# A hybrid encoder layer on one core: attention's steps spread wider, linear attention's set closer, and rests issued a step behind

## The chip, the core and the metric

The kernel runs on one core of a Trainium2 chip. The core has five engines that run side by side, each through its own queue in order: TensorE (PE in the profile, with its weight loads as PEld), VectorE (DVE), ScalarE (ACT), GpSimd (POOL) and SyncE (SP). The last two issue DMA transfers here; POOL also fills a few tiles. Engines wait for each other through semaphores. The metric is device time in microseconds from start to end of one execution; before the change it is 2229.53 us, the median of 3 runs (2229.45 to 2230.32).

## What is computed

One layer over 512 tokens with 2048 features, all in 32-bit floats. Half of the mixing width is attention with three (window, dilation) patterns merged by their softmax denominators (16 heads of 64), the other half gated linear attention in both directions (4 heads, keys of 128, values of 256). Then an output projection, a SwiGLU block and norms.

```python
h = rmsnorm(x, attn_norm_w[l])
proj = h @ w_in[l]
aq, ak, av, gq, gk, gv, gr, glr = jnp.split(proj, split_idx, axis=-1)
attn = mixture_of_dilations(_heads(aq, 16), _heads(ak, 16), _heads(av, 16), rel_bias_table)
log_a_f = jax.nn.log_sigmoid(lr_f @ gla_gate_w_fwd[l] + gla_gate_b_fwd[l]) / 16.0
...
o = gla_causal(qh, kh, vh, log_a_f) + flip(gla_causal(flip(qh), ..., flip(log_a_b)))
o = o * lax.rsqrt(jnp.mean(o * o, axis=-1, keepdims=True) + 1e-6)
gla_out = (_merge_heads(o) * gla_norm_w[l]) * jax.nn.silu(gr)
x = x + jnp.concatenate([attn_out, gla_out], axis=-1) @ w_out[l]
h = rmsnorm(x, ffn_norm_w[l])
x = x + (jax.nn.silu(h @ w_gate[l]) * (h @ w_up[l])) @ w_down[l]
```

## The kernel before

Every large product is made in a rounded 32-bit format in three passes. An operand is split into a rounded part (a cast, on ScalarE) and a rest (operand minus rounded part, on VectorE), and TensorE multiplies rounded by rounded, rounded by rest and rest by rounded (L321 to L323, or L330 to L332).

**Weights** come through the `Stream`. SP loads pieces of 128 x 1024 from `in_w_in` and other weights (L207); a piece is two halves of 512 columns. `split` makes the rounded part (L222) and the rest (L223) of each half ahead of its use, gives the raw piece back after its second half, and loads the next. At most three raw pieces are held.

**Jobs.** A job is one projection of 512 columns: 16 halves, and for each half 12 matmuls of 512 columns into four PSUM banks (four banks, three passes). At the start of half i, `run_job` splits up to half i + 2, so rounded part and rest of a half are issued two halves ahead. At a job's end `evac` empties the four banks: `evac_gqk` (L787, L790, on VectorE), `evac_gv` (L816, on ScalarE), `evac_gr` (L830 on VectorE, L835 on ScalarE, then `gla_out`, L844, on VectorE).

**Six jobs in the middle** make the linear attention's q and k (pair 0), v (pair 0), q and k (pair 1), v (pair 1) and two gates. While they run, smaller work is woven in as generators that yield after every step. `side` holds them in a queue: the low-rank gate product, then attention, then the linear attention of heads 0 and 1 (`two` lets the two alternate), then of heads 2 and 3. A later one begins when the one ahead of it is done. A job's `rate` says how many side steps go with each half; with `fine` set they are spread over the half's four groups of three matmuls. Before every side step one step of `urgent` runs. The rate is 2.9 in all six jobs. `slow` adds an empty step after each step of the low-rank product and of linear attention.

**Attention** goes in 64 units (16 heads, four blocks of 128 queries), two steps a unit, with the stages of five units overlapped. For unit u: scores (TensorE, L593 and L594), add bias and take the extreme (`att_max`, VectorE, L603), exponential with its sum (`att_exp`, ScalarE, L611), reciprocal and scaling (`att_norm`, VectorE, L615 and L616), transposes into PSUM (TensorE, L621), rounding (`att_round`, ScalarE, L629), rest (`att_rest`, VectorE, L635), product with the values (TensorE, L645 and L646, every second unit), a lift and an add (`att_lift`, ScalarE, L655, and `att_mix`, VectorE, L664). When a pair of heads is done, `split_of` splits the result (L387, L388). The 8 PSUM banks are shared: four belong to the job, the rest serve scores, transposes and products in turn.

`read_qk(pr)` has POOL read q and k of a pair of heads back from device memory (`qkd`, L535, eight transfers); `load_qk(pr)` scales and splits them: a ScalarE activation (L547, L552) and a VectorE rest (L548, L553) for each of four tiles, rest right behind its activation.

**Linear attention** of one head has 14 steps: gates (TensorE, L866), for each direction a log-sigmoid (ScalarE L876 to L878, VectorE L879, L880), for each direction a scan and its exponents (VectorE L888 to L903, ScalarE L901) and then scaled q and k (ScalarE L907, L908; VectorE L910, L911), products and transposes of them (TensorE L929, L935; VectorE L940, ScalarE L945, VectorE L949), states (TensorE L963, ScalarE L975, VectorE L977), an empty step, outputs (TensorE L999, ScalarE L1002), normalisation (L358 to L364, L1012 on ScalarE), transposes (TensorE L1018, VectorE L1021).

**Just before the six jobs** the attention's own q and k projections run in another form (`Front`, seven products of half size, L1392 and L1406, with casts L1310 and rests L1315). Its last unit is emptied by `evac7` (nine ScalarE copies, L1432 to L1440, and VectorE adds, L1426 and L1427). At the second of its last four pieces `read_qk(0)` is issued, at the third `load_qk(0)` goes to the head of `urgent`, and a step of `urgent` runs after each piece.

Of the kernel before, what the change touches and what calls it, by code (L numbers as in the profile page):

```python
# [16 lines left out]
F32R = mybir.dt.float32r  # L17
U32 = mybir.dt.uint32
AF = mybir.ActivationFunctionType
OP = mybir.AluOpType  # L20
# [98 lines left out]
def layer(nc, tc, x, attn_norm_w, w_in, rel_table, gw_f, gb_f, gw_b, gb_b, gla_norm_w, w_out,  # L119
# [7 lines left out]
    with tc.manual_schedule(), \  # L127
# [52 lines left out]
        class Stream:  # L180


            def __init__(self):
                self.pieces = []
                self.halves = []
                self.n_dma = self.n_conv = 0
                self.limit = 3
                self.held = 0
                self.until = None
                self.big = None  # L190
                self.keep = 0

            def add(self, pieces):
# [6 lines left out]
            def load(self):  # L200
                last = len(self.pieces) if self.until is None else self.until
                while self.n_dma < last and self.held < self.limit and s4.free:
# [5 lines left out]
                    self.n_dma += 1  # L208

            def split(self, upto):  # L210
                end = len(self.halves) if self.until is None else 2 * self.until
                while self.n_conv < min(upto, end):
                    h = self.halves[self.n_conv]
                    if self.n_dma <= h[0]:
                        self.load()
                    raw = self.pieces[h[0]][1]
                    r = raw.t[:, h[1] * 512:(h[1] + 1) * 512]
                    if self.big is not None and self.n_conv >= self.big and len(s4.free) > 3:
                        h[2], h[3] = s4.pair()
                    else:  # L220
                        h[2], h[3] = hilo(self.keep)
                    act.copy(h[2].t, r)  # L222
                    dve.tensor_tensor(h[3].t, r, h[2].f, op=OP.subtract)  # L223
                    self.n_conv += 1
                    if h[1] == 1:
                        put(raw)
                        self.held -= 1
                        self.load()

# [64 lines left out]
        def run_job(j):  # L294
# [6 lines left out]
            for i in range(j.n):  # L301
# [5 lines left out]
                if j.tail is not None:  # L307
                    j.before(i)
                _, _, wh, wl = st.halves[j.first + i]
                ks = j.kts[i * per:(i + 1) * per]  # L310
# [226 lines left out]
        def load_qk(pr):  # L537


            qs, ks = qkr.pop(pr)  # L540
            sign = (-1.0, 1.0)[pr % 2]
            QK[pr] = []
            for n in range(2):
                v = lambda x_: x_.rearrange("p (b c) -> p b c", c=P)
                e, low = s2.get(F32R), slice(64, 128)
                src, scale = v(qs[n].f)[:, :, ::-1], -sign * DH ** -0.5
                act.activation(v(e.t), src, AF.Copy, scale=scale)  # L547
                dve.scalar_tensor_tensor(v(e.t)[low], src[low], scale, v(e.f)[low], op0=OP.mult, op1=OP.subtract)  # L548
                put(qs[n])
                yield  # L550
                k = s2.get(F32R)
                act.activation(k.t, ks[n].f, AF.Copy, scale=sign)  # L552
                dve.scalar_tensor_tensor(ks[n].t, ks[n].f, sign, k.f, op0=OP.mult, op1=OP.subtract)  # L553
                QK[pr].append((e, k, ks[n]))
                yield
            ready.add(pr)
# [56 lines left out]
        def att_norm(u):  # L613
            L = AT[u]
            dve.reciprocal(ar[u % 4], asum[u % 4])  # L615
            dve.tensor_scalar(L.t, L.t, ar[u % 4], None, op0=OP.mult)  # L616

# [39 lines left out]
        def att_mix(v):  # L657
# [10 lines left out]
            if v % 4 == 3:  # L668
                mixh[pr] = split_of(mixf.pop(pr))

        def attention():
# [5 lines left out]

            for u in range(UNITS + 5):
                h = u // 4
                if u < UNITS:  # L680
# [4 lines left out]
                    while h // 2 not in ready:  # L685
                        run_urgent()
                run(att_scores, u)
                run(att_exp, u - 1)
                run(att_round, u - 3)
# [121 lines left out]
        def evac_gv(pr):  # L811
            def f(banks):
# [305 lines left out]

        def before_first(i):
            if i == 2:  # L1120
                load_v(0)

        n_front = len(jobs)
        RATE = 2.9
        for pr in range(2):
            seg = [(w_in, C_GQ + pr * 256), (w_in, C_GK + pr * 256)]
            job("A", [piece512(seg, None, k) for k in range(0, KT, 2)], list(range(KT)), acts_h,
                evac_gqk(pr), rate=RATE, start=gstart if pr == 0 else None,
                before=None if pr else before_first, limit=3)
            job("B", [piece512(w_in, C_GV + pr * 512, k) for k in range(0, KT, 2)], list(range(KT)), acts_h,  # L1130
                evac_gv(pr), rate=RATE)

        for pr in range(2):
            job("A", [piece512(w_in, C_GR + pr * 512, k) for k in range(0, KT, 2)], list(range(KT)), acts_h,
                evac_gr(pr), rate=RATE)
        n_in = len(jobs)
# [397 lines left out]
        class Front(Feed):  # L1534
# [18 lines left out]
            def run(self):  # L1553
                banks = {}
                for i, (u, q) in enumerate(self.seq):
# [12 lines left out]
                    if u == len(self.units) - 1:  # L1568
# [485 lines left out]
```

## Time and profile before

| | |
|---|---|
| median of 3 runs | 2229.53 us (2229.45 to 2230.32) |
| the profiled execution | 2232.89 us, of which the span of the trace is 2231.1 |
| TensorE busy | 2180.0 us (98%) |
| VectorE busy | 1786.4 us (80%) |
| ScalarE busy | 1180.2 us (53%) |
| GpSimd busy | 332.1 us (15%) |
| mean granted clock of TensorE | 0.993 |

A row of the timeline gives the start in us from the span's start, how long it took, engine, line, operation, what it writes and reads, and how many were merged; in brackets, how long the engine had been idle before and what ended that. A row of the waits gives who waited for whom: us in total, how often, the longest. A row of a stretch gives its length and for each engine the busy time and the number of instructions, then the granted clock of TensorE, the DMA engines' busy share and GB/s. A row of a group gives busy us and the mean ns of one, then idle us of the engine before it and what ended that. Lines such as L593 are those of the kernel before. Matmuls are pipelined, so the busy time of TensorE isn't its peak.

### The profile page before, as it was taken

The numbers are of one execution on the slowest core, as the hardware profiler recorded it, in microseconds if no ns is written. First come the engines' busy times: TensorE is split into PE (matmuls) and PEld (weight loads), VectorE is DVE, ScalarE is ACT, GpSimd is POOL, SyncE is SP. The second block draws the span as 40 slices with busy tenths as digits, with TensorE's granted clock in tenths as the row PEclk, the third lists the DMA queues.
The fourth block names the chain that finished last, engine by engine and source line by source line (L and its number), as shares of the span: only waits on it lengthen the run. The fifth ranks groups of instructions, "written<-read, shape, count | busy, mean of one in ns | idle before, by whom it ended". The sixth has DMA issues, their size and how long they took to land.

```text
span 2231.1 us, 34599 instructions
## 1 busy us (share of the span) xinstructions
PE 2180.0 (98%) x12618; PEld 1907.8 (86%) x12618; DVE 1786.4 (80%) x3104; ACT 1180.2 (53%) x2165; POOL 332.1 (15%) x462
## 2 busy tenths in 40 slices
PE   9999898998999999999999999999999999999998
PEld 7888777777878888988888888888888899999987
DVE  5699668777664676799898999999898888988885
ACT  7454345565554444455555555555555655555562
POOL 0011221110000110012121211212121120011300
PEclk9999999999999999999999999999999999999999
DMA  5367763443323885257767776766777886566982
GB/s 187 123 188 176 188 204 115 143 138 120 124 85 108 306 292 190 86 153 188 179 184 182 174 199 170 190 179 182 182 177 196 242 194 199 184 181 154 276 315 76
DMA packets 257368, 397.81 MB, mean 178 GB/s; under 512 B 18925, under 2 KB 154269, under 8 KB 257198
## 3 DMA queue, kind: packets, MB, share of 16 engines
q1 hardware_dynamic: 203134, 276.69, 38.7%
q0 software_dynamic: 53744, 118.39, 23.8%
q8 instruction: 99, 1.62, 0.3%
q14 instruction: 71, 0.58, 0.1%
q10 hardware_dynamic: 320, 0.53, 0.1%
HBM read 285.37 MB, written 64.29 MB: 157 GB/s over the span
## 4 chain that ended last, share of the span: by engine, by line
PE 54%; DMA 1%; DVE 1%; issue 1%; ACT 0%; POOL 0%; DVEq 0%; POOLq 0%; ACTq 0%
PE ps L1406 24%; PE ps L1392 12%; PE ps L1755 5%; PE ps L1756 5%; PE ps L1754 5%; PE ps L330 1%; PE ps L331 1%; PE ps L332 1%; DMA gd<-b 1%; DMA b<-a 1%; PE ps L1949 0%; PE ps L1948 0%; PE ps L1950 0%; DVE b L1315 0%; DVE a L1625 0%
## 5 line engine op out<-in xcount | busy, mean ns | idle before, releaser
L1310 ACT CAST b<-b 128x768 fp32r<-128x768 f32 (+1 forms) x537 | 489.0, 945 | 335.0 <-DVE b L1315 142.0
L1315 DVE TENSOR_TENSOR b<-b,b 128x768 fp32r<-128x768 f32 (+1 forms) x537 | 563.8, 1084 | 32.4 <-ACT b L1310 20.3
L1406 PE MATMUL ps<-b,b 128*128 128x512 f32 x1552 | 451.0, 393 | 0.4 <-ACT b L1310 0.2
L1406 PE MATMUL ps<-a,b 128*128 128x512 f32 x1248 | 365.6, 394 | 3.3 <-DVE b L1426 3.3
L1406 PEld LDWEIGHTS ps<-b,b 128*128 128x128 f32 x1552 | 263.5, 188 | 30.7 <-ACT b L1310 0.7
L1392 PEld LDWEIGHTS ps<-b,b 128*128 128x128 f32 x1552 | 252.8, 190 | 36.1
L1392 PE MATMUL ps<-b,b 128*128 128x256 f32 x1552 | 275.5, 280 | 0.0
L1392 PEld LDWEIGHTS ps<-a,b 128*128 128x128 f32 x1248 | 208.0, 189 | 34.2 <-DVE b L1315 0.5
L1406 PEld LDWEIGHTS ps<-a,b 128*128 128x128 f32 x1248 | 207.3, 189 | 23.2 <-ACT a L1438 3.8
L1392 PE MATMUL ps<-a,b 128*128 128x256 f32 x1248 | 223.7, 280 | 0.0
L1297 DVE TENSOR_TENSOR b<-b 128x512 f32<-128x512 f32 x244 | 167.4, 686 | 19.0 <-DMA b<-in_w_down_dram 7.1
L1754 PE MATMUL ps<-b,b 128*128 128x256 f32 x624 | 176.6, 283 | 0.0
L1756 PE MATMUL ps<-b,b 128*128 128x256 f32 x624 | 176.6, 283 | 0.0
L1755 PE MATMUL ps<-b,b 128*128 128x256 f32 x624 | 176.6, 283 | 0.0
L223 DVE TENSOR_TENSOR b<-b,b 128x512 fp32r<-128x512 f32 x171 | 114.9, 686 | 69.8 <-ACT b L222 69.8
L330 PE MATMUL ps<-b,b 128*128 128x512 f32 x392 | 156.4, 399 | 2.2 <-ACT b L222 2.2
L331 PE MATMUL ps<-b,b 128*128 128x512 f32 x392 | 154.1, 393 | 0.9 <-DVE b L223 0.9
L332 PE MATMUL ps<-b,b 128*128 128x512 f32 x392 | 154.0, 393 | 0.0
L222 ACT CAST b<-b 128x512 fp32r<-128x512 f32 x171 | 100.8, 618 | 41.8 <-PE ps L332 27.7
L1755 PEld LDWEIGHTS ps<-b,b 128*128 128x128 f32 x624 | 119.8, 192 | 0.0
L1756 PEld LDWEIGHTS ps<-b,b 128*128 128x128 f32 x624 | 119.8, 192 | 0.0
L1754 PEld LDWEIGHTS ps<-b,b 128*128 128x128 f32 x624 | 119.8, 192 | 0.0
(295 smaller groups left out, 4289.8 us busy)
## 6 DMA issues: line engine op xcount, KB each, us to landing
b<-in_w_gate_dram SPq DMA_DIRECT2D x109, 512.0 KB, 4.2
b<-in_w_up_dram SPq DMA_DIRECT2D x88, 512.0 KB, 4.3
b<-in_w_down_dram SPq DMA_DIRECT2D x88, 512.0 KB, 8.0
b<-in_w_in_dram SPq DMA_DIRECT2D x78, 512.0 KB, 3.8
b<-a POOLq DMA_DIRECT2D x150, 256.0 KB, 4.5
b<-in_w_out_dram SPq DMA_DIRECT2D x32, 512.0 KB, 5.7
gd<-b POOLq DMA_DIRECT2D x22, 512.0 KB, 3.9
b<-gd SPq DMA_DIRECT2D x22, 512.0 KB, 8.1
```

Source lines behind the costliest of these rows:

```text
L223: dve.tensor_tensor(h[3].t, r, h[2].f, op=OP.subtract)
L330: mm(o, xh.t[:, c], wh.t[:, w], start=first and not on, stop=False, skip_group_check=on)
L331: mm(o, xh.t[:, c], wl.t[:, w], start=False, stop=False, skip_group_check=on)
L332: mm(o, xl.t[:, c], wh.t[:, w], start=False, stop=last, skip_group_check=on)
L1297: dve.tensor_tensor(s_[:, :, 0:2], r[:, :, 1:3], r[:, :, 0:1].to_broadcast(shape), op=OP.add)
L1310: act.copy(o, src)
L1315: dve.tensor_tensor(o, src, h, op=OP.subtract)
L1392: mm(o, wl, xh, start=False, stop=end, skip_group_check=True)
L1406: mm(o.rearrange("p (s t) -> p s t", s=2), wh, x_, start=first and p == 0, stop=False, skip_group_check=True)
L1754: mm(o, xh[:, t], wh, start=first and h == 0, stop=False, skip_group_check=True)
L1755: mm(o, xh[:, t], wl, start=False, stop=False, skip_group_check=True)
L1756: mm(o, xl[:, t], wh, start=False, stop=last, skip_group_check=True)
```

## The change

1. The six jobs' rate of 2.9 becomes 2.5 for the first four (`RATES[0]`) and 2.0 for the two gate jobs. Linear attention loses the empty steps that `slow` put in; the low-rank product keeps them.
2. `load_qk(0)` goes to the head of `urgent` at the second half of the first job instead of the third of the last four front pieces.
3. In the six jobs (`st.lag = j.fine`) the rest of a weight half is issued by the next step's `split`, ahead of that step's cast, instead of right behind its own cast; the raw piece goes back, and its successor is loaded, a step later.
4. `load_qk` issues each rest a step behind its activation: one activation a step, four steps, the last rest behind the fourth.
5. Odd units' scaling leaves `att_norm` for a new `att_scale` on ScalarE, ahead of the next exponential, in the step before their transposes. Even units' scaling and all reciprocals stay on VectorE.
6. The split of a finished pair of heads moves from `att_mix` to the start of the next unit.

```diff
@@ Stream
+            def rests(self, upto):
+                while self.open and self.open[0] < upto:
+                    n = self.open.popleft()
+                    h = self.halves[n]
+                    raw = self.pieces[h[0]][1]
+                    dve.tensor_tensor(h[3].t, raw.t[:, h[1] * 512:(h[1] + 1) * 512], h[2].f, op=OP.subtract)
+                    if h[1] == 1:
+                        put(raw)
+                        self.held -= 1
+                        self.load()
+
             def split(self, upto):
+                self.rests(len(self.halves))
...
                     act.copy(h[2].t, r)
-                    dve.tensor_tensor(h[3].t, r, h[2].f, op=OP.subtract)
+                    self.open.append(self.n_conv)
                     self.n_conv += 1
-                    if h[1] == 1:
-                        put(raw)
-                        self.held -= 1
-                        self.load()
+                    if not self.lag:
+                        self.rests(self.n_conv)
@@ run_job
+                st.lag = j.fine
+                st.rests(j.first + i + 1)
@@ load_qk
+            for m in range(5):
+                if m:
+                    _, hf, src, lo, scale, r, done = todo[m - 1]
+                    dve.scalar_tensor_tensor(lo, src[r], scale, hf[r], op0=OP.mult, op1=OP.subtract)
+                    if done:
+                        put(done)
+                if m < 4:
+                    act.activation(todo[m][0], todo[m][2], AF.Copy, scale=todo[m][4])
+                    yield
@@ attention
         def att_norm(u):
-            L = AT[u]
             dve.reciprocal(ar[u % 4], asum[u % 4])
-            dve.tensor_scalar(L.t, L.t, ar[u % 4], None, op0=OP.mult)
+            if u % 2 == 0:
+                dve.tensor_scalar(AT[u].t, AT[u].t, ar[u % 4], None, op0=OP.mult)
+
+        def att_scale(u):
+            if u % 2:
+                act.activation(AT[u].t, AT[u].t, AF.Copy, scale=ar[u % 4])
...
-                mixh[pr] = split_of(mixf.pop(pr))
+                at["mix"] = pr
...
+                if "mix" in at:
+                    pr = at.pop("mix")
+                    mixh[pr] = split_of(mixf.pop(pr))
                 run(att_scores, u)
+                run(att_scale, u - 2)
                 run(att_exp, u - 1)
                 run(att_round, u - 3)
@@ evac_gv
-                side.append(slow(two(gla(2 * pr), gla(2 * pr + 1))))
+                side.append(two(gla(2 * pr), gla(2 * pr + 1)))
@@ before_first, jobs
+            if i == 1:
+                urgent.appendleft(load_qk(0))
...
-        RATE = 2.9
+        RATES = (2.5, 2.0)
@@ Front.run
-                            urgent.appendleft(load_qk(0))
```

More of the change, by code (lines that the diff above doesn't have):

```diff
@@ L191, in __init__ @@
                 self.keep = 0
+                self.lag = False
+                self.open = deque()
             def add(self, pieces):
@@ L542, in load_qk @@
             QK[pr] = []
+            v = lambda x_: x_.rearrange("p (b c) -> p b c", c=P)
+            low = slice(64, 128)
+            todo = []
             for n in range(2):
[L544 to L553, printed above, removed]
-                QK[pr].append((e, k, ks[n]))
-                yield
+                e, k = s2.get(F32R), s2.get(F32R)
+                todo += [(v(e.t), v(e.f), v(qs[n].f)[:, :, ::-1], v(e.t)[low], -sign * DH ** -0.5, low, qs[n]),
+                         (k.t, k.f, ks[n].f, ks[n].t, sign, slice(0, 128), None)]
+                QK[pr].append((e, k, ks[n]))
+            for m in range(5):
[7 more added lines that the diff above has]
+                    yield
             ready.add(pr)
@@ L676, in run @@
                     f(u)
-            for u in range(UNITS + 5):
+            for u in range(UNITS + 6):
                 h = u // 4
@@ L1127, in layer @@
             job("A", [piece512(seg, None, k) for k in range(0, KT, 2)], list(range(KT)), acts_h,
-                evac_gqk(pr), rate=RATE, start=gstart if pr == 0 else None,
+                evac_gqk(pr), rate=RATES[0], start=gstart if pr == 0 else None,
                 before=None if pr else before_first, limit=3)
             job("B", [piece512(w_in, C_GV + pr * 512, k) for k in range(0, KT, 2)], list(range(KT)), acts_h,
-                evac_gv(pr), rate=RATE)
+                evac_gv(pr), rate=RATES[0])
         for pr in range(2):
             job("A", [piece512(w_in, C_GR + pr * 512, k) for k in range(0, KT, 2)], list(range(KT)), acts_h,
-                evac_gr(pr), rate=RATE)
+                evac_gr(pr), rate=RATES[1])
         n_in = len(jobs)
```

## The prediction

> **What bounds the kernel now.** I read the page first: its head and engine rows.
>
> ```profile
> span 2231.1 us, 34599 instructions
> PE 2180.0 (98%) x12618; PEld 1907.8 (86%) x12618; DVE 1786.4 (80%) x3104; ACT 1180.2 (53%) x2165; POOL 332.1 (15%) x462
> ```
>
> TensorE (PE) is idle for 51 us of the span, so a change that only reorders work can win that and the time at a lowered clock, no more. Next, the busy time by stretches, cut where the diff acts: the end of the front products, the stage with attention, the one with linear attention alone.
>
> ```profile
> core 0: us, PE busy (x) PEld busy (x) DVE busy (x) ACT busy (x) POOL busy (x), PEclk, DMA share, GB/s
> ...
> 272.00:282.00 10.00, 0.60 (x2) 0.50 (x2) 4.00 (x10) 4.85 (x14) 4.24 (x8) 0.72 1.07 287
> 282.00:288.00 6.00, 5.94 (x17) 4.10 (x16) 5.94 (x11) 3.64 (x8) 0.00 (x0) 0.62 1.04 357
> ...
> 449.00:457.00 8.00, 7.40 (x33) 5.98 (x34) 6.62 (x16) 5.28 (x12) 2.97 (x7) 0.79 0.82 268
> ...
> 540.00:548.00 8.00, 5.00 (x19) 4.12 (x18) 5.25 (x13) 4.09 (x9) 0.00 (x0) 0.66 0.46 182
> ...
> 556.00:724.00 168.00, 165.23 (x797) 138.84 (x796) 94.92 (x174) 87.51 (x193) 7.36 (x14) 1.00 0.34 106
> ```
>
> Then who made TensorE wait, in 306 to 556 us (attention) and in 556 to 724 us (linear attention alone):
>
> ```profile
> PE ps L593 <- DVE b L635: 12.6, 12, 3.0
> PE ps L621 <- DVE a L616: 2.9, 5, 1.0
> PE ps L621 <- ACT b L816: 2.7, 1, 2.7
> PE ps L621 <- DVE a L790: 2.6, 2, 1.8
> ```
>
> ```profile
> PE ps L929 <- DVE a L911: 2.0, 1, 2.0
> PE ps L1018 <- ACT b L1012: 0.7, 2, 0.4
> ```
>
> Three places, then: a hole of over 9 us at 272; 20.8 us of waits in attention, plus clock losses of 0.21 x 8 + 0.34 x 8 = 4.4 us; 2.7 us in linear attention. The rest of the span has little to give.
>
> **Part 1: load_qk(0) goes from the last front products to the second step of the first projection job.** The timeline of ScalarE, and TensorE's row after the hole:
>
> ```profile
> 276.93 0.63 ACT L547 ACTIVATE a<-a 128x512 fp32r<-128x512 f32 x1 [13.60 <-DMA a<-qkd]
> 277.47 0.35 ACT L1432 COPY a<-ps 128x256 f32<-128x256 f32 x1
> ...
> 279.56 0.46 ACT L1440 COPY a<-ps 128x256 f32<-128x256 f32 x1
> 280.25 0.63 ACT L552 ACTIVATE a<-a 128x512 fp32r<-128x512 f32 x1 [0.22 <-DMA a<-qkd]
> 280.78 1.12 ACT L222 CAST b<-b 128x512 fp32r<-128x512 f32 x2
> ```
>
> ```profile
> 271.65 0.39 PE L1392 MATMUL ps<-b,b 128*128 128x256 f32 x2
> 281.44 0.79 PE L321 MATMUL ps<-b,b 128*128 128x512 f32 x1 [9.39 <-ACT b L222]
> ```
>
> ScalarE sits 13.6 us on a DMA that only attention needs; queued behind it are the nine evacuation copies and the first weight cast, for which TensorE waits. In the changed order the copies follow the products bank by bank. The last two still come after 272.05 (0.26 us apart), then the cast (0.62): TensorE resumes near 273.5, idle 1.5 us instead of 9.4: 7.9 saved. Over 282 to 288 it ran 17 matmuls; at full clock, with weight matmuls alone, the view by stretches has
>
> ```profile
> 573.00:589.00 16.00, 16.00 (x72) 13.23 (x72) 15.00 (x28) 7.09 (x17) 1.07 (x2) 1.00 0.33 96
> ```
>
> 72 in 16 us, 0.22 each, 2.7 us for the twelve of a half. The loss of 6 - 17 x 0.22 = 2.2 us goes with the hole. Sum **-10 us**. What is late next: load_qk(0)'s four activations now stand in front of the cast for the fifth half. That cast is needed only after four halves of 2.7 us plus the low-rank matmuls, after 284; the first k read had landed at 280.25. The eight POOL reads are not moved. Bounds: 0 (the reads slip by 6 us) to -11.
>
> **Part 2: attention at 2.5 steps a half, odd scalings on ScalarE, rests a step behind.** What the rate is worth depends on what sets the pace. Three units as the timeline has them (L603 max, L611 exponential, L629 rounding, L635 rest, L222/L223 weight cast and rest):
>
> ```profile
> 403.29 0.68 DVE L603 CUSTOM_DVE_ANT_0 a<-ps,b 128x512 f32<-128x512 f32 x1
> ...
> 404.07 0.72 ACT L611 ACTIVATE a<-a,small 128x512 f32<-128x512 f32 x1 [0.39 <-DVE small L603]
> 404.45 0.16 DVE L615 RECIPROCAL small<-small 128x1 f32<-128x1 f32 x1
> ...
> 404.79 0.57 ACT L629 CAST b<-ps 128x512 fp32r<-128x512 f32 x1
> ...
> 406.38 0.68 DVE L603 CUSTOM_DVE_ANT_0 a<-ps,b 128x512 f32<-128x512 f32 x1
> ...
> 409.51 0.69 DVE L223 TENSOR_TENSOR a<-b,a 128x512 fp32r<-128x512 f32 x1 [1.85 <-ACT a L222]
> ...
> 410.72 0.68 DVE L603 CUSTOM_DVE_ANT_0 a<-ps,b 128x512 f32<-128x512 f32 x1
> ```
>
> This is a ring between two engines: max, exponential (0.78 later), rounding (0.72), rest and next max (0.60 each, the pace of the two instructions from 409.51 to 410.72), 2.7 us with nothing in the way. A weight rest ahead of L635 makes it 3.09 (403.29 to 406.38); one that waits for its cast, queued behind rounding, 4.34 (406.38 to 410.72). The lag takes away these waits, 35 us (20.6 + 14.3), and the scaling leaves VectorE for every second unit:
>
> ```profile
> L616 DVE TENSOR_SCALAR a<-a,small 128x512 f32<-128x512 f32 x64 | 31.2, 487 | 2.3
> L223 DVE TENSOR_TENSOR a<-b,a 128x512 fp32r<-128x512 f32 x33 | 22.7, 689 | 20.6 <-ACT a L222 20.6
> L223 DVE TENSOR_TENSOR b<-b,b 128x512 fp32r<-128x512 f32 x16 | 11.0, 689 | 14.3 <-ACT b L222 14.3
> ...
> L816 ACT ACTIVATE b<-ps,small 128x512 f32<-128x512 f32 x8 | 4.9, 698 | 0.0
> ```
>
> VectorE loses 32 x 0.487 = 15.6 us; ScalarE gains 32 x 0.698 = 22.3 (no activation from SBUF with a column as scale is in the trace; L816, from PSUM, is the nearest). The new activation stands ahead of the next exponential, and for that unit it needs max, mix and reciprocal first: 404.61 instead of 404.07, then 0.62, so that ring takes 2.7 + 1.2 = 3.9. The mean of 2.7 and 3.9 is 3.3, with load_qk and the mix splits some 3.5. TensorE's own unit is 3.4 us of work now (306 to 556 less 25.2, over 64 units and about two of start and end); 2/2.5 - 2/2.9 = 0.11 more halves of 2.7 us in it make 3.7. So TensorE sets the pace, narrowly. The lost time of 20.8 + 4.4 = 25 us should fall to what the job ends cause (L816 and L790: 5.3, part of L593's, some clock): **-18 us**. Bounds: 0 if the ring stays slower than TensorE, -25 if all goes. Releasing raw weights a step later delays SP's next load by one half; three pieces of two halves are held, so I take nothing: two pieces still held, some 11 us of work, hide it (without that cover a cast could come one half, 2.7 us, late).
>
> The Trainium skill's page "ScalarE: Activation LUTs", section "Rules for kernel authors", says to do plain multiplies on VectorE, not ScalarE. The rows agree on price, 487 against 698 ns; by the rule alone the move loses 6.7 us.
>
> **Part 3: linear attention without its empty steps, 2 steps a half.** Here the cover disappears. Its first half, gate to L929, is a chain through ScalarE and VectorE that ends just as TensorE wants it:
>
> ```profile
> 562.97 0.69 ACT L876 ACTIVATE a<-ps,wcol 128x512 f32<-128x512 f32 x1 [0.29 <-PE ps L866]
> ```
>
> ```profile
> 588.03 0.68 DVE L911 TENSOR_TENSOR a<-a,a 128x512 f32<-128x512 f32 x1
> ```
>
> ```profile
> 589.37 1.95 PE L929 MATMUL ps<-a,a 128*128 128x128 f32 x16
> ```
>
> ```profile
> 639.10 0.69 ACT L876 ACTIVATE a<-ps,wcol 128x512 f32<-128x512 f32 x1 [1.60 <-PE ps L866]
> ```
>
> For the first pair of heads (rows at 562, 588 and 589) the chain takes 25.7 us (562.97 to 588.71) and TensorE came to L929 0.66 us after its end. In the changed record seven halves lie between, not nearly ten: 7 x 2.7 + 0.5 = 19.4 us. The chain loses two weight rests (1.2) and a few waits (0.5), but four L816 evacuations of the fourth job, which wait for that job's last matmul, now fall into its ScalarE part: +3.9. So 28 against 19.4: **+8.5 us** of stall. TensorE meets part of it early, since weight rests issued a step later leave one half of slack, not two. The second pair went from 639.10 to the L911 that ends TensorE's wait, around the evacuation of the fifth job:
>
> ```profile
> 669.26 1.16 PE L929 MATMUL ps<-a,a 128*128 128x128 f32 x8 [2.00 <-DVE a L911]
> ```
>
> Thirty us less 0.5, against 7.25 halves and 0.5, 20: 9.5 of stall instead of 2.0, **+7.5**. At the end the two heads' last scalings follow 4.19 us apart:
>
> ```profile
> 630.19 1.57 ACT L1012 ACTIVATE b<-ps,small 128x256 f32<-128x256 f32 x4 [0.83 <-DVE small L364]
> ...
> 634.38 1.57 ACT L1012 ACTIVATE b<-ps,small 128x256 f32<-128x256 f32 x4 [0.83 <-DVE small L364]
> ```
>
> TensorE's transposes for them now stand half a half (1.4) and eight transposes (half of the L929 row's 1.95) apart: 1.8 late, and the first, with 1.5 halves behind its own chain, I put at 0.8. Two pairs, less the 0.7 there is: **+4.5**. A stall near 5 us after the fifth job's evacuation may cost clock; I take +0.5 (0 to 4). Sum **+21**, bounds +6 (half of each chain hides) to +27.
>
> **The sum**: -10 - 18 + 21 = -7. The profiled execution took 2232.89 us (span 2231.1 and 1.8 around it), 3.4 above the median of 2229.53; the difference applied to the median gives **2222 us**.
>
> **Rivals.** *Linear attention hides most* (the chain's ScalarE and VectorE parts overlap better than in line): for it, VectorE is busy 94.92 of the 168 us of that stage; against it, the 0.66 us margin and its 15.00 of 16 us from 573 on. Part 3 is +8: 2210. *The ring becomes the bound, and it ends slower*: the ScalarE scaling in front of the exponential adds 1.2 us to every second unit; from a mean ring of 3.7 us on, attention gains nothing. For it: the mean leaves only 0.2 us, and ScalarE's casts and loads share its gaps; against it, 35 us of cast waits vanish. -10 + 0 + 21 = +11: 2240. *The front hole only moves*: ScalarE waits for the same reads a step later, and the fifth half's cast is late; against it the row at 280.25. Part 1 is 0: 2232. *The clock falls*: after the 9.39 us hole the granted clock was 0.62 and after 2.7 us of waiting 0.79, while the 2.00 at 669 cost nothing. If both pairs' stalls do that, 2 x 2.5 us (as at 540): 2227.
>
> The Trainium skill's "TensorE: Matmul & The Clock Gate", Part 1, has the clock halve after an idle window of about 3.4 us; the 0.79 after a shorter wait does not quite fit that.
>
> **How the numbers follow.** Forecast 0.38, good hiding 0.22, ring 0.25, moved hole 0.08, clock 0.07. A measurement of this kernel can tell about 0.2%, 4.5 us. The forecast, with 7 us of spread either way, is faster in 0.65 of its chance and same in most of the rest; good hiding is faster; the ring slower in three quarters; the moved hole about the same; the clock split. Faster 0.53, same 0.21, slower 0.26. The range reaches from -30 (attention -25, linear attention +6) to +11: 2200 to 2240; the forecast's own is 2212 to 2232.
>
> **What would show it.** Right: TensorE's first L321 near 273.5 with a wait under 3 us; no L223 waiting for L222 in attention, and L593's wait on L635 under 5 us; L929 or the weight matmuls waiting for L911 and L223, some 15 us in the last two jobs. Wrong: attention transposes waiting for the new activation, waits on L635 as large as now, or linear attention without stalls.

## The result, and the profile after

| | before | after |
|---|---|---|
| median | 2229.93 us (2229.45 to 2232.07) | 2209.71 us (2208.75 to 2212.47) |
| profiled execution, its span | 2232.89, 2231.1 | 2209.98, 2208.2 |
| TensorE idle (span less busy) | 51.1 us | 36.6 us |

The medians are of runs taken side by side on one chip. The ratio is 0.991, 95% interval 0.9892 to 0.9927: 20 us faster. The forecast was 2222, its range 2200 to 2240; the direction was right, the size was not. Lines from here on are those of the kernel after: the job's matmuls are L336 to L338 and L345 to L347, weight cast L237 and rest L218, scores L612, max L622, exponential L630, odd scaling L639 on ScalarE, transposes L644, rounding L652, rest of it L658, evacuations L817 and L843 of the jobs, linear attention L903 (gate), L938, L956, L1039, L1045.

The page's head and engine rows, after:

```profile
span 2208.2 us, 34604 instructions
PE 2171.6 (98%) x12618; PEld 1906.9 (86%) x12618; DVE 1771.8 (80%) x3072; ACT 1201.4 (54%) x2197; POOL 332.9 (15%) x462
```

Of the 22.9 us between the two spans, 14.5 are idle time of TensorE and 8.4 are busy time: the same 12618 matmuls took less long. Not all of it is the change's. One and the same transfer near the end of the front, before anything that the diff touches, in the timeline of GpSimd, before and after:

```profile
260.48 0.86 POOL L1452 DMA_DIRECT2D b<-a  x1 [3.89 <-DVE b L1297]
```

```profile
257.61 0.86 POOL L1481 DMA_DIRECT2D b<-a  x1 [3.89 <-DVE b L1326]
```

The profiled execution of before was 2.9 us late already here, much as it was above its median. The change has some 20 us to answer for. By stretches, after (length, busy time of each engine with its instructions, clock, DMA share, GB/s):

```profile
272.00:282.00 10.00, 5.44 (x17) 4.24 (x18) 5.62 (x12) 6.75 (x17) 3.74 (x7) 0.66 1.05 281
306.00:556.00 250.00, 247.36 (x1330) 208.21 (x1329) 181.37 (x422) 172.25 (x361) 34.90 (x67) 1.00 0.49 147
556.00:724.00 168.00, 156.79 (x733) 128.88 (x732) 107.01 (x203) 90.69 (x201) 9.11 (x17) 0.98 0.40 128
```

The hole before the first job is smaller but still there, attention is nearly without gaps at full clock, and linear attention has gaps that it did not have. What TensorE waited for in the last two stretches (in all, times, longest):

```profile
PE ps L612 <- DVE b L658: 1.7, 3, 0.8
PE ps L644 <- ACT a L639: 0.9, 1, 0.9
```

```profile
PE ps L338 <- DVE b L218: 8.6, 5, 4.4
PE ps L346 <- DVE b L218: 0.8, 1, 0.8
PE ps L956 <- DVE a L938: 0.8, 1, 0.8
PE ps L1045 <- ACT b L1039: 0.8, 2, 0.4
```

Attention's waits went from 20.8 us to 2.6, linear attention's from 2.7 to 11.0. One part of the gain is in no row of waits. Groups of TensorE in 306 to 556 us with shapes kept apart (busy us, mean ns), before and then after:

```profile
L621 PE MATMUL ps<-idn,a 128*128 128x128 f32 x256 | 39.7, 278 | 8.9 <-DVE a L616 2.9 <-ACT b L816 2.7 <-DVE a L790 2.6
L593 PE MATMUL ps<-a,a 128*128 128x512 f32 x64 | 27.6, 431 | 12.9 <-DVE b L635 12.6
```

```profile
L644 PE MATMUL ps<-idn,a 128*128 128x128 f32 x256 | 38.4, 272 | 1.0 <-ACT a L639 0.9
L612 PE MATMUL ps<-a,a 128*128 128x512 f32 x63 | 25.2, 400 | 1.7 <-DVE b L658 1.7
```

A score matmul is 31 ns shorter, a transpose 6. With each group's difference times its count after, over the groups found in both, that makes some 9.5 us, of which 4.4 are the clock. The other 5 I take for matmuls that a wait had drawn out. Their cause is not shown; their size is borne out by the six jobs as a whole, which run from 281.44 to 725.94 us before and from 276.56 to 702.41 after. That is 18.7 us less, of which 11.3 are idle time of TensorE and 2.6 lowered clock (mean 0.983 before, 0.988 after); the rest is in neither.

The front, after: ScalarE's timeline from the second evacuation copy on, then TensorE's, then GpSimd's:

```profile
266.43 0.37 ACT L1462 COPY a<-ps 128x256 f32<-128x256 f32 x1 [1.02 <-PE ps L1421]
273.97 0.37 ACT L1463 COPY a<-ps 128x256 f32<-128x256 f32 x1 [7.17 <-DMA b<-a]
...
275.83 1.20 ACT L237 CAST b<-b 128x512 fp32r<-128x512 f32 x2
```

```profile
276.56 0.80 PE L336 MATMUL ps<-b,b 128*128 128x512 f32 x1 [7.38 <-ACT b L237]
```

```profile
264.61 1.21 POOL L1484 DMA_DIRECT2D b<-a  x1
265.15 3.82 POOL L550 DMA_DIRECT2D a<-qkd  x6
```

The first two copies follow their products, as forecast. The third waits 7.17 us for a transfer out of SBUF, and with it the casts and TensorE. Its destination is a buffer that the unit before still feeds to an accumulating transfer (L1484, issued at 264.61, 9.3 us to landing): four of the pool's buffers had just gone to `read_qk(0)` (L550).

### The profile page after: what moved, and what is told of

The parts are those of the page before. It is cut to its first block, busy times and chain, and to the rows that moved or that the text cites. A ratio compares the mean times of both kernels' runs of the same rounds, so it can differ in the third digit from the quotient of the medians.

```text
span 2208.2 us, 34604 instructions
## 1 busy us (share of the span) xinstructions
PE 2171.6 (98%) x12618; PEld 1906.9 (86%) x12618; DVE 1771.8 (80%) x3072; ACT 1201.4 (54%) x2197; POOL 332.9 (15%) x462
## 4 chain that ended last, share of the span: by engine, by line
PE 81%; issue 8%; DVE 4%; DMA 4%; ACT 2%; POOL 1%; DVEq 0%; ACTq 0%; SPq 0%; POOLq 0%
PE ps L1435 25%; PE ps L1421 13%; PE ps L346 5%; PE ps L345 5%; PE ps L347 5%; PE ps L1784 5%; PE ps L1783 5%; PE ps L1782 5%; DMA b<-a 3%; PE ps L338 2%; PE ps L336 2%; PE ps L337 2%; PE ps L644 1%; PE ps L1026 1%; DVE b L1344 1%
## 5 line engine op out<-in xcount | busy, mean ns | idle before, releaser
L1435 PE MATMUL ps<-b,b 128*128 128x512 f32 x1552 | 451.0, 393 | 0.4 <-ACT b L1339 0.2
L345 PE MATMUL ps<-b,b 128*128 128x512 f32 x380 | 151.5, 399 | 2.0 <-ACT b L237 2.0
L346 PE MATMUL ps<-b,b 128*128 128x512 f32 x380 | 149.1, 392 | 0.8 <-DVE b L218 0.8
L347 PE MATMUL ps<-b,b 128*128 128x512 f32 x380 | 148.9, 392 | 0.0
L218 DVE TENSOR_TENSOR b<-b,b 128x512 fp32r<-128x512 f32 x176 | 117.8, 685 | 26.1 <-ACT b L237 26.0
L237 ACT CAST b<-b 128x512 fp32r<-128x512 f32 x176 | 104.2, 620 | 40.5 <-PE ps L347 19.0
```

The costliest lines, as they stand in the source:

```text
L218: dve.tensor_tensor(h[3].t, raw.t[:, h[1] * 512:(h[1] + 1) * 512], h[2].f, op=OP.subtract)
L345: mm(o, xh.t[:, c], wh.t[:, w], start=first and not on, stop=False, skip_group_check=on)
L346: mm(o, xh.t[:, c], wl.t[:, w], start=False, stop=False, skip_group_check=on)
L347: mm(o, xl.t[:, c], wh.t[:, w], start=False, stop=last, skip_group_check=on)
L1435: mm(o.rearrange("p (s t) -> p s t", s=2), wh, x_, start=first and p == 0, stop=False, skip_group_check=True)
```

## The experiments

**Two switches, four kernels: the lag of the weights' rests, and the engine of the odd scaling.** The kernel after has the lag and scales odd units on ScalarE. No lag:

```diff
-                st.lag = j.fine
+                st.lag = False
```

> The changed kernel (2209.7 us) with every weight rest right behind its own cast again; rates, load_qk and the odd scaling as changed. Theory 1 (the lag is what frees attention's ring, and it costs in linear attention, where rests have one half of slack in place of two): L223 waits some 30 us for its cast in attention and TensorE waits there 10 us more than the about 4 of the changed kernel; in the last two jobs TensorE's waits for weight rests, 9 us and 3 of clock, shrink by 8 or more. Sum 2207 to 2214. Theory 2 (the lower rate alone frees attention): attention as in the changed kernel, within 3 us, and only the gain in linear attention is left: 2199 to 2203.

Measured 2238.11 us (2235.93 to 2240.34), ratio to before 1.0041 (1.0029 to 1.0054): slower than the kernel before, and 28 us above the kernel after. Both ranges missed it. With the lag kept, all scalings on VectorE:

```diff
-            if u % 2 == 0:
-                dve.tensor_scalar(AT[u].t, AT[u].t, ar[u % 4], None, op0=OP.mult)
+            dve.tensor_scalar(AT[u].t, AT[u].t, ar[u % 4], None, op0=OP.mult)
...
-                run(att_scale, u - 2)
```

> The changed kernel with all scalings on VectorE, 32 x 0.487 = 15.6 us more there in attention, and 32 activations fewer on ScalarE. Theory 1 (the ring max, exponential, rounding, rest sets attention's pace, and the scaling on ScalarE only lengthens it for odd units, by 1.2 us): attention's waits stay below 6 us, the time within 3 us: 2207 to 2212. Theory 2 (VectorE's occupancy was the bound, so that moving the scaling is what pays): 10 us or more of waits return in attention: 2219 or more.

2210.82 us (2208.84 to 2213.05), 0.992 (0.9908 to 0.9933), in the range of the first theory: the scaling's engine makes no difference here. Then both edits together:

```diff
-                st.lag = j.fine
+                st.lag = False
...
-            if u % 2 == 0:
-                dve.tensor_scalar(AT[u].t, AT[u].t, ar[u % 4], None, op0=OP.mult)
+            dve.tensor_scalar(AT[u].t, AT[u].t, ar[u % 4], None, op0=OP.mult)
...
-                run(att_scale, u - 2)
```

> The kernel after with st.lag = False and with all 64 scalings on VectorE. Without the lag and with the odd scalings on ScalarE the time was 2238.11, with waits in attention of 11.8 us at L612 for L658 and 2.8 at L644 for L639; with the lag the engine of the scaling made no difference (2210.82 against 2209.71). Theory 1: the ring of max, exponential, rounding and rest is the pace again once the weight rests stand in it ahead of their casts, and there the ScalarE scaling ahead of the exponential costs, as the prediction had it: with the scalings on VectorE the L612 waits fall to 7 us or less and the time to 2228 to 2234. Theory 2: the scaling is beside the ring in either case, L612's waits stay at 10 us or more: 2236 to 2240.

2219.22 us (2216.73 to 2221.04), 0.995 (0.9936 to 0.9964), beyond both ranges. So:

| median, us | odd scaling on ScalarE | all on VectorE |
|---|---|---|
| rests a step behind | 2209.71 | 2210.82 |
| rests behind their casts | 2238.11 | 2219.22 |

The scaling costs 19 us without the lag and nothing with it. Waits of TensorE in 306 to 556 us without the lag, first with the odd scaling on ScalarE and then with all on VectorE:

```profile
PE ps L612 <- DVE b L658: 11.8, 15, 2.0
PE ps L644 <- ACT a L639: 2.8, 7, 0.9
```

```profile
PE ps L612 <- DVE b L657: 3.1, 4, 1.3
```

An odd unit without the lag, scaling on ScalarE: VectorE's timeline, then ScalarE's:

```profile
404.41 0.68 DVE L622 CUSTOM_DVE_ANT_0 a<-ps,b 128x512 f32<-128x512 f32 x1
...
408.30 0.69 DVE L218 TENSOR_TENSOR a<-b,a 128x512 fp32r<-128x512 f32 x1 [2.54 <-ACT a L237]
409.02 0.69 DVE L658 TENSOR_TENSOR b<-ps,b 128x512 fp32r<-128x512 f32 x1
409.63 0.68 DVE L622 CUSTOM_DVE_ANT_0 a<-ps,b 128x512 f32<-128x512 f32 x1
```

```profile
405.84 0.72 ACT L639 ACTIVATE a<-a,small 128x512 f32<-128x512 f32 x1 [1.69 <-DVE small L633]
406.47 0.71 ACT L630 ACTIVATE a<-a,small 128x512 f32<-128x512 f32 x1
...
407.18 0.56 ACT L652 CAST b<-ps 128x512 fp32r<-128x512 f32 x1
407.64 0.62 ACT L237 CAST a<-b 128x512 fp32r<-128x512 f32 x1
```

Max to max takes 5.22 us. Scaling, exponential, rounding and weight cast follow each other on ScalarE, and VectorE, empty for 2.54 us, waits for the last of them with a weight rest that nobody needs yet; L658 and the next max stand behind it. With the lag that link is cut. The cast waits alone don't cost this, though: with all scalings on VectorE and no lag, VectorE waits 32.3 us for weight casts in 306 to 556 us (16.4 and 15.9 by tile), nearly the 35 of before, and TensorE only 3.1 for L657. VectorE's groups in 306 to 556 us, after (the last columns: idle before, and what ended it):

```profile
L658 DVE TENSOR_TENSOR b<-ps,b 128x512 fp32r<-128x512 f32 x64 | 44.2, 691 | 46.2 <-ACT b L652 45.4
L218 DVE TENSOR_TENSOR a<-b,a 128x512 fp32r<-128x512 f32 x35 | 23.8, 680 | 0.1
```

The weight rest waits for nothing. VectorE still idles 46 us in front of L658, yet TensorE waits only 1.7 us for it: the ring has room.

**The pieces alone.** The kernel before with nothing but the weights' lag:

```diff
@@ Stream, run_job as in the kernel after
+                st.lag = j.fine
+                st.rests(j.first + i + 1)
```

> The kernel before with the lag of the weights' rests alone: old rates and empty steps, load_qk, its place and the scaling as before. Theory 1 (the cast waits of L223 in the ring are most of what attention loses): 2214 to 2222, TensorE's waits in attention 20.8 down to 8 to 14. Theory 2 (the lag pays only at the lower rate): 2225 to 2230.

2220.52 us (2218.44 to 2222.11), 0.9955 (0.9943 to 0.9967): some 9 us of gain, in the range of its first theory. Lines there are a few lower (L608, L636 and L650 are L612, L644 and L658). Waits for L650 fall to 4.8 us in 306 to 556; those at the ends of jobs stay (another 2.6 for the evacuation on VectorE):

```profile
PE ps L608 <- DVE b L650: 4.8, 5, 1.6
PE ps L636 <- ACT b L831: 2.7, 1, 2.7
```

The kernel before with only the rates 2.5 and 2.0 and no empty steps:

```diff
-        RATE = 2.9
+        RATES = (2.5, 2.0)
...
-                side.append(slow(two(gla(2 * pr), gla(2 * pr + 1))))
+                side.append(two(gla(2 * pr), gla(2 * pr + 1)))
```

> The kernel before with the new rates and without linear attention's empty steps, nothing else. Theory 1 (without the lag the ring is slower than TensorE even at 2.5 steps, and linear attention's denser chain costs 15 to 20 us): 2236 to 2246, slower than before. Theory 2 (the rate alone frees attention): attention's waits fall below 8 us, 2220 to 2230.

2233.21 us (2229.16 to 2235.45), 1.0012 (1.0004 to 1.002), 3 us of loss and in neither range: attention's waits halve, linear attention's (below, 556 to 724 us; L944 and L926 are L956 and L938) take it back.

```profile
PE ps L944 <- DVE a L926: 7.2, 2, 5.0
PE ps L336 <- ACT b L237: 2.8, 2, 2.0
```

The kernel after with the old rates (2.9, 2.9 and the empty steps):

```diff
-        RATES = (2.5, 2.0)
+        RATES = (2.9, 2.9)
...
-                side.append(two(gla(2 * pr), gla(2 * pr + 1)))
+                side.append(slow(two(gla(2 * pr), gla(2 * pr + 1))))
```

> The changed kernel with 2.9 steps a half in all six jobs and the empty steps of linear attention back. Theory 1 (the lag frees the ring, which at about 3.5 us a unit then nearly keeps up with TensorE's 3.4): attention waits 8 to 15 us, linear attention 3 in place of about 15: 2205 to 2213. Theory 2 (the lower rate is what did it): attention's waits and clock losses are back at 25 us, less what the lag gives (below 5), linear attention gains 14: 2215 to 2225.

2215.30 us (2213.23 to 2216.02), 0.9938 (0.9925 to 0.995). With all else in place the rates are worth 5.6 us. The time just falls into the second theory's range; the waits in attention, 11.6 us, are what the first expected. Linear attention then waits 3.6 us, but attention has waits again where a job's end meets a unit's transposes (306 to 556 us):

```profile
PE ps L644 <- ACT a L639: 5.2, 6, 3.3
PE ps L644 <- ACT b L843: 2.7, 1, 2.7
```

**Linear attention: is the lag a cost there?** The lag in the first four jobs only:

```diff
-                st.lag = j.fine
+                st.lag = j.fine and j.rate > 2.2
```

> The changed kernel with the lag in the first four jobs alone. Theory 1 (one half of slack is too little in the two gate jobs): the waits for weight rests near 565 and 635 us shrink from about 9 us and 3 of clock to 3 or less: 2200 to 2204. Theory 2 (the chain of scans is late anyway, and what TensorE doesn't wait for at the weight rests it waits for at L911's result, named L938 in the changed kernel): the waits move there and the time stays within 3 us: 2207 to 2212.

2217.95 us (2216.83 to 2219.23), 0.9952 (0.9939 to 0.9966). Both theories missed: the lag gains some 7 us in the gate jobs too. Waits in 556 to 724 us:

```profile
PE ps L956 <- DVE a L938: 9.4, 2, 5.0
PE ps L1045 <- ACT b L1039: 2.7, 3, 1.3
PE ps L338 <- DVE b L218: 1.9, 4, 1.0
PE ps L336 <- ACT b L237: 1.5, 3, 0.8
```

15.5 us against 11.0 after. The spans of the two traces differ by 7.9 us. Of these the two gate jobs have 7.1 (557.13 to 711.41 us here, 555.20 to 702.41 after): 4.5 more of waits, some 1.7 of clock (0.97 against 0.98), and 0.9 left over. Another 1.7 stand already at the first job's start (278.25 against 276.56), which the lag of the gate jobs can't touch, and behind the jobs this run was 1.1 faster. TensorE met the two chains at L956 for 9.4 us in all. With the lag it meets them mostly at the weights' rest instead.

**The front.** `load_qk(0)` back at the front's third of its last four pieces, all else as after:

```diff
-            if i == 1:
-                urgent.appendleft(load_qk(0))
...
                         if q == 2:
                             gla_operands()
+                            urgent.appendleft(load_qk(0))
```

> The changed kernel with load_qk(0) back at the third of the last front pieces. Theory 1 (its activations waited until 276.9 for the reads, the copies would in any case have waited to about 274 for their buffer, so that moving it was worth only the difference): TensorE's wait near 270 us is 9 to 10 in place of 7.4, with the clock 2211 to 2214. Theory 2 (moving it was worth the 10 us of the prediction and the copies' wait is a new one that the change makes): 2217 or more.

2216.63 us (2215.79 to 2217.45), 0.9938 (0.9926 to 0.9949), between the two ranges: the move is worth 7 us, not 2 as the two holes (9.39 and 7.38) suggest. Its timeline of ScalarE shows why:

```profile
276.66 0.63 ACT L573 ACTIVATE a<-a 128x512 fp32r<-128x512 f32 x1 [15.71 <-DMA a<-qkd]
...
281.01 0.63 ACT L573 ACTIVATE a<-a 128x512 fp32r<-128x512 f32 x1 [1.25 <-DMA a<-qkd]
281.54 1.64 ACT L237 CAST b<-b 128x512 fp32r<-128x512 f32 x3
```

Both activations stand ahead of the casts, as before, and their reads land within 0.8 us of the times they did there (276.93 and 280.25), though this execution's front was over 2 us ahead; TensorE waited 12.5 us.

The lag has a part in this hole, in every trace. TensorE's wait before the first job, in us, one execution of each kernel:

| | no lag | lag |
|---|---|---|
| `load_qk(0)` at its old place | 9.39 (before), 9.27 (rates alone) | 12.29 (lag alone), 12.52 (this run) |
| `load_qk(0)` in the first job | 6.41 (no lag), 6.30 (no lag, all on VectorE) | 7.38 (after), 6.91 to 7.39 (three more) |

With the lag the eight reads took 10.7 to 11.5 us from issue to landing (median in each trace), without it 8.4 to 8.8. SP's order there differs: the four loads of the attention's values (L581) go out ahead of a piece of weights instead of behind it (265.27 us in the kernel after, 267.85 in the one without the lag). That this order delays the reads is likely but not shown. So the move is worth 3 us of waiting without the lag and 5 with it, and the lag costs 3 and 1.

Now the reads themselves later, and `load_qk(0)` with them:

```diff
-                        if q == 1:
-                            read_qk(0)
...
-            if i == 1:
-                urgent.appendleft(load_qk(0))
+            if i == 0:
+                read_qk(0)
+            if i == 3:
+                urgent.appendleft(load_qk(0))
```

> The changed kernel with the eight reads of q and k (read_qk(0)) behind the last front unit's evacuation, at the first step of the first job, and load_qk(0) at its fourth step. Theory 1 (the third evacuation copy waits until 273.97 for a buffer that the unit before's last accumulating transfer, landed at 273.90, still reads; the reads had taken the older free buffers): copies follow the products, TensorE waits 1 to 3 us there in place of 7.4 and keeps its clock: 2201 to 2205. Theory 2 (transfers are the bound there, their engines being nearly all busy from 262 to 286 us): the casts wait for weights in place of the copies, TensorE's wait stays above 5: 2207 to 2211.

2205.65 us (2203.18 to 2206.55), 0.989 (0.9874 to 0.9905), just above the first theory's range: the hole is nearly gone, and this is the fastest kernel of the study.

```profile
266.09 0.38 ACT L1465 COPY a<-ps 128x256 f32<-128x256 f32 x1
...
269.14 1.15 ACT L237 CAST b<-b 128x512 fp32r<-128x512 f32 x2
...
280.67 0.63 ACT L573 ACTIVATE a<-a 128x512 fp32r<-128x512 f32 x1 [7.69 <-DMA a<-qkd]
```

The third copy (L1465 here) comes at once, the cast at 269.14 instead of 275.83, and TensorE waits 1.3 us. The accumulating transfer (L1486 here) still takes 8.8 us to land, so it is the buffer that was freed, not the transfer that got faster. The first q activation waits 7.69 us for its read; behind it TensorE waits only 1.8 us more up to 306.

**Can the steps be divided better?** On top of that kernel, two other pairs of rates.

```diff
-        RATES = (2.5, 2.0)
+        RATES = (2.6, 1.7)
```

> The kernel with read_qk(0) and load_qk(0) later (2205.65), and RATES (2.6, 1.7) in place of (2.5, 2.0). Theory 1: linear attention at 2 steps a half is what costs now; in that kernel TensorE waited 9.4 + 0.9 us at L338 for the weight's rest L218 behind the state chain on VectorE, 1.0 at L956, 0.8 at L346 and 0.8 at L1045, all but a few us of it in the last two jobs, and the clock fell to 0.91 after one of them. With 0.3 step a half less the chain gets 18% more matmul work beside it: the L338 wait falls to about 5 us, the clock loss goes, attention's waits grow by at most 2: 2199 to 2203. Theory 2: the chain's length is the same, only other matmuls wait for it (L956 in place of L338), and attention at 2.6 steps brings back waits at L612: 2204 to 2209.

2210.32 us (2209.94 to 2212.61), 0.9921 (0.9907 to 0.9934), above both ranges. And (2.8, 1.5):

```diff
-        RATES = (2.5, 2.0)
+        RATES = (2.8, 1.5)
```

> As the run at (2.6, 1.7), with RATES (2.8, 1.5): the same number of steps in all, moved further to attention. Theory 1 (linear attention's density costs, attention's up to 2.8 costs little while the rests lag): L338's wait under 3 us, attention's waits 4 to 8 us: 2198 to 2203. Theory 2 (TensorE's pace and the ring of max, exponential, rounding and rest are near each other, so 2.8 is past the knee as 2.9 was, which cost 5.6 us): attention's waits 10 us and more, 2205 to 2212.

2209.35 us (2208.35 to 2211.13), 0.9913 (0.9899 to 0.9926), as the second theory had it. Neither beats 2.5 and 2.0. The interval of the first lies just above that of the fastest kernel, that of the second overlaps it. Waits in 306 to 556 us, at 2.6 and at 2.8:

```profile
PE ps L644 <- DVE a L817: 2.9, 1, 2.9
PE ps L644 <- ACT b L843: 1.1, 1, 1.1
```

```profile
PE ps L612 <- DVE b L658: 5.1, 6, 1.3
PE ps L346 <- DVE b L218: 4.6, 2, 3.3
```

At 2.6 a job's end meets attention's transposes again, and L338 still waits 8.9 us in linear attention. At 2.8 the waits for the ring return, and a weight rest is late where the two stages meet; linear attention itself waits only 1.2 us in 556 to 724. The first theory was right about that stage at 1.5 steps and wrong about attention at 2.8.

**Where the time went, by stage.** Lengths in us in one execution of each kernel: TensorE's wait before the first job, then from the first matmul of job 1 to that of job 5, and from there to the first matmul behind job 6. The rates decide which steps fall into which jobs, so the last two columns compare only among rows of the same rates.

| kernel | rates | wait before | four jobs | two gate jobs |
|---|---|---|---|---|
| before | 2.9 | 9.4 | 312.6 | 131.9 |
| lag alone | 2.9 | 12.3 | 297.4 | 131.5 |
| rates alone | 2.5, 2.0 | 9.3 | 292.7 | 155.1 |
| after, no lag, all scalings on VectorE | 2.5, 2.0 | 6.3 | 281.0 | 153.9 |
| after, all scalings on VectorE | 2.5, 2.0 | 6.9 | 278.6 | 147.3 |
| after, no lag | 2.5, 2.0 | 6.4 | 300.7 | 153.6 |
| after | 2.5, 2.0 | 7.4 | 278.6 | 147.2 |
| after, reads late | 2.5, 2.0 | 1.3 | 278.6 | 147.2 |

With all scalings on VectorE the lag gains 2.4 us in the four jobs and 6.6 in the gate jobs: at these rates it pays mostly in linear attention. On the kernel before, with 2.9 steps and the other rests not late, it gains 15.2 in the four jobs. What the odd scaling on ScalarE costs without the lag, 19.7 us, lies wholly in the four jobs. And between the third row and the fourth, which differ by the rests of q and k, the mix's split and the place of `load_qk(0)`, the four jobs get 11.7 us shorter: issuing the other rests late seems to pay as it does for the weights' (the three were not tried apart).

## Why the prediction came out as it did

**Part 1, the front: -10 forecast.** In the trace of after it is -2.5: the hole fell from 9.39 to 7.38 us, and of the 5.44 us in which TensorE ran before 282, 17 matmuls at 0.22 are 3.7, so 1.7 us of slow clock stay (from 2.2). The step that failed is "the copies follow the products bank by bank": two did, the third had a second wait behind the one moved away, for the buffer under L1484. The row of before showed it only indirectly, since ScalarE stood at the earlier wait until later. A second step was the "nothing" taken for loads that the lag issues later: the lag made this hole 3 us longer with the load in its old place and 1 us with it moved. The price of an open front, 10 us, was near 2216.63 (load in its old place) less 2205.65 (reads and load late), which is 11, but by other terms: the wait there fell by 11.3 us, from a hole that the lag had made longer, and the six jobs took 425.8 us in both traces, so the 2.2 us of clock did not show in the time. "What is late next" was right too: the fifth half's cast was not late.

**Part 2, attention: -18 forecast, about -28 in the trace.** Waits -18.2 and clock -4.4 make -22.6, and another 5, which the sum did not count, are in neither. Three steps were off. The waits that the forecast left standing at the ends of jobs (L816, L790, 5.3 us) nearly vanished; the old rates on the kernel after and (2.6, 1.7) bring them back, so they seem to hang on where a job's end falls in a unit, which no sum of durations gives. "TensorE sets the pace, narrowly" was too cautious with the lag: the ring of 3.9 us for an odd unit made no difference to the time. The new activation took 723 ns, not 698, and it is the lag that makes it free. And the 35 us of VectorE's waits for casts were taken for the pace of attention. They are it only together with something else: on the kernel before, or with the odd scaling on ScalarE, where the odd unit took 5.22 us without the lag. At 2.5 steps with all scalings on VectorE 32.3 us of them stay and TensorE hardly feels it: its waits in attention fell from 20.8 to 9.8 us by the rates alone, to 4.0 with the other rests late and the load moved, and to 2.0 with the lag. The rival in which the ring decides describes the kernel without the lag; that 2238 is near its 2240 is luck, since that rival kept the lag.

By the Trainium skill's page "ScalarE: Activation LUTs", section "Rules for kernel authors", the move of a plain multiply to ScalarE was to lose. Here it gave 1 us or nothing with the lag (2209.71 against 2210.82) and lost 19 without: where the multiply stands decided, not its 487 or 723 ns.

**Part 3, linear attention: +21 forecast, about +11 in the trace.** Waits rose by 8.3 us, and the one long wait cost clock:

```profile
632.00:640.00 8.00, 4.36 (x10) 3.47 (x11) 7.74 (x14) 5.92 (x11) 0.00 (x0) 0.68 0.00 1
```

0.32 x 8 is 2.6 us. The places were right, the sizes of the chains not. The chains put at 8.5 and 7.5 us stalled TensorE for 5.0 (four waits at L338 in 561 to 575 us and the one at L956) and 4.4; with no lag there they did so too, 9.4 in all at L956. The tails, put at +4.5, cost 0.8 where 0.7 had stood before; without the lag they cost 2.7, so that step left out that weight rests no longer wait for casts in front of the heads' last instructions. VectorE idled 14.1 us for weight casts in 535 to 680 us with the lag in the first four jobs only, and not at all with it in all six. Where the forecast treated the lag here only as slack lost, it was a gain of some 7 us.

**The sum.** -2.5, -28 and +11 are -19.5, near the 20 measured; the forecast had -10, -18 and +21. Its errors in parts 1 and 2 pulled against each other, part 3 carried the miss: good hiding, a rival with +8 for part 3, is nearest to what linear attention did. That its 2210 is the measured time is partly luck, since its parts 1 and 2 were off by +7.5 and -10. The clock fell as the clock rival had it, once instead of twice. Step by step the medians go: the rates alone lose 3 us, the other rests and the move of `load_qk(0)` then gain 14 (2233.21 to 2219.22), the weights' lag 8 (to 2210.82), the odd scaling 1 or nothing. The lag alone on the kernel before gains 9, so these parts nearly add up, though they fall into other stages; it is the lag and the engine of the scaling that don't add.

The profiled execution at (2.6, 1.7) has 6.6 us more span than that at (2.5, 2.0) with late reads. Of these 1.8 stand already before the first job, 4.1 are in the six jobs (429.9 against 425.8), with 2.2 more idle time and a lower clock (0.988 against 0.996), and 0.7 come behind. Open stays how the gain of the other rests divides between q and k, the mix and the move of `load_qk(0)`: they were tried only together.

## What to carry to other kernels

Where two engines hand work back and forth in order, an instruction that is needed by nobody yet but waits for the other engine can set the pace; issue it a step later before counting busy time, and price every other edit with that link cut, since the same edit cost 19 us or nothing. But an engine's waits are not yet a loss: 32 us of them cost the four jobs 2.4 us with the scaling on VectorE. When a wait is moved off an engine, ask of each instruction behind it what it would wait for next: the buffer it writes and the transfers that still read it. The new rates lost 3 us alone and gained 5.6 once such links were gone, and the best rate must be tried: a tenth of a step more in attention and three tenths less behind it cost 4.7 us here (2210.32 against 2205.65).

## What the runs showed of the hardware

An accumulating SBUF transfer of 128 KB (L1484) took 9.3 us from issue to landing while the reads of q and k and the weights ran beside it, and an evacuation copy that was to write its source waited until then. The granted clock did not follow a wait's length alone. With rates (2.6, 1.7) one wait of 2.9 us in attention, behind one of 0.7, left it at 0.92 over 20 us; in the kernel after, four waits of 0.55 to 1.54 us, 4.2 in all within 13 us, left it at 1.00. These are one execution each. The rows of the two stretches:

```profile
480.00:500.00 20.00, 16.36 (x79) 12.77 (x78) 14.23 (x32) 10.69 (x25) 2.19 (x4) 0.92 0.44 133
```

```profile
560.00:576.00 16.00, 11.78 (x48) 8.47 (x47) 14.61 (x27) 7.01 (x15) 0.28 (x1) 1.00 0.26 89
```

The Trainium skill's "TensorE: Matmul & The Clock Gate", Part 1, has the clock halve after an idle window of some 3.4 us. The 0.68 behind the wait of 4.4 us agrees with that, the 0.92 does not quite: 0.08 x 20 is 1.6 us lost behind 2.9 us of waiting and a shorter wait.
